# One encoder layer on one core: elementwise work taken from GpSimd, low-rank products in full passes

## The chip, the core and the metric

One core of a Trainium2 chip runs the whole layer as one program. Its engines work side by side, each on its own queue of instructions in order: TensorE (PE, with its weight loads PEld), VectorE (DVE), ScalarE (ACT), GpSimd (POOL) and SyncE (SP), which issues the DMAs. The metric is the device time of one execution in microseconds. Before the change it is 4108.12 us, median of three runs (4107.86 to 4108.83).

## The reference, cut to what matters

Two sequences (2048 and 256 tokens, width 1024, float32) run through one layer: RMSNorm, one projection to 3328 columns, half of which feed differential attention and half a two-directional RWKV-7 recurrence, an output projection and a squared-ReLU MLP. The parts that the change touches:

```python
q = apply_rope(rms_norm(q, q_norm_g), cos, sin)          # the same for k
p = softmax(q k^T * scale)                               # two maps per head
attn = p[:, :, 0] - lam * p[:, :, 1]; o = attn @ v

zf = zf + mu_prev * (z_prev - zf) + mu_next * (z_next - zf)
w_log = -softplus(-(w0 + tanh(w_dn) @ w_up)) - 0.5;  decay = exp(-exp(w_log))
a_rate = sigmoid(a0 + a_dn @ a_up);  g = sigmoid(g_dn) @ g_up
kk = k * k_k / norm(k * k_k);  k_dir = k * (1 + (a_rate - 1) * k_a)
# w_up, a_up: rank 64 to 512 channels, for two directions
# state = state * w_t + (state a_t) b_t + v_t k_t;  y = state r_t
bonus = sum(r * k_dir * r_k) * v
```

## The kernel before, in words

The 2304 tokens are 18 tiles of 128 rows. Four stages follow one another, with some overlap.

**Projection and mixer preparation (0 to about 1026 us).** `project_stream` walks over column groups of 256 in a fixed order. Every product is three float32r passes (`mm3`, lines 100 to 102: high by high, low by high, high by low). Mixer columns are made transposed (`tall`), attention columns with tokens on the partitions (`wide`, two token tiles at a time). A wide tile of q or k goes through `rope` (lines 325 to 373): squares on ScalarE, their sum on VectorE, the power -0.5 on GpSimd (`rsqrt`, line 90), the product with it on VectorE (qn), then the rotation: t1 on GpSimd (L346), one half of t2 on VectorE and one on GpSimd (L349), the sum (L353), a split into two parts (L355, L356), transposes on TensorE (L363) and the stores. Tiles qn, t1 and the shared buffer of rsq and t2 are single, so one rope tile follows another.

Beside it `rw_prep` (line 717) prepares the recurrence for two token tiles at a time: nine blocks, each with four chunks of 128 channels. A block mixes neighbouring tokens (`mix`, L737 to L739), splits the 64 + 64 low-rank rows (wa) into a high and a low part (L747, L748) and, for each chunk and direction, multiplies them with w_up and a_up (L813): the w half on partitions 0 to 63, the a half on 64 to 127, three products of 64 rows for each. Tanh follows (L815), an affine map on GpSimd (L816), a running sum along time (L819), two exponentials (L822, L823), and the operands aro and kb of the recurrence: the products L831, L846, L847 and L853 and the map L844 on GpSimd, the rest on VectorE (L834, L841, L843, L854). Preparation steps are put between projection steps by a rate (PREP_RATE). Within a stage the order of the instructions on each engine is settled when the program is built, by a planner that simulates the engines with its own costs.

**Attention beside the recurrence (about 1026 to 2222 us).** `attn_stream` takes one head and one tile of 128 queries at a time; the long sequence has four blocks of 512 keys for each of the two maps. `attn_scores`: two score products (L601, L602) into one of three PSUM buffers, the row maximum on VectorE (L604), the exponential on ScalarE (L608). `attn_combine` brings the four blocks to one maximum: map 0 is rescaled, blocks 0 and 1 on ScalarE (L631), 2 and 3 on GpSimd (L633); map 1 is multiplied and added, blocks 0 and 2 in one VectorE operation (L639), 1 and 3 in two on GpSimd (L636, L637). `attn_pv` transposes and multiplies with the values one query tile later. The recurrence (`rw_units`: inter, leaf, merge, chain) is put between by a ratio; its leaf (L954, L956) has part of its steps on GpSimd.

**wout and MLP (2222 to 4106 us).** Not touched by the change.

Of the kernel before, what the change touches and what calls it, by code (L numbers as in the profile page):

```python
# [22 lines left out]
CDEC = -0.5 * float(np.exp(-0.5))  # L23
# [34 lines left out]
class K:  # L58
# [266 lines left out]
    def rope(self, ps, t, m, c0):  # L325

        nc, sp, pp = self.nc, self.pj, self.pjp
        CW = self.CW
        part, g0, n = c0 // 512, (c0 % 512) // 64, CW // 64
        gcs = sp.tile([128, m, 128], F32, name="gcs", tag="gcs")  # L330
        runs = [0] + [j for j in range(1, m) if self.pos[t + j] != self.pos[t + j - 1] + 1] + [m]
        for j0, j1 in zip(runs, runs[1:]):
            p0 = self.pos[t + j0] * 128
            nc.sync.dma_start(out=gcs[:, j0:j1], in_=self.cst[part, p0:p0 + (j1 - j0) * 128].rearrange("(n p) c -> p n c", p=128))
        sq = sp.tile([128, m * n, 64], F32, name="rsq", tag="rsq", bufs=RSQ)
        z = ps.rearrange("p m (a b) -> p (m a) b", b=64)
        nc.scalar.activation(out=sq, in_=z, func=AF.Square)
        ss = sp.tile([128, m * n], F32, name="rss", tag="rss")
        nc.vector.tensor_reduce(out=ss, in_=sq, axis=AX.X, op=ALU.add)
        rs = sp.tile([128, m * n], F32, name="rrs", tag="rrs")  # L340
        self.rsqrt(rs, ss, 1.0 / 64, 1e-6)
        qn = sp.tile([128, m * n, 64], F32, name="qn", tag="qn", bufs=1)
        nc.vector.tensor_tensor(out=qn, in0=z, in1=rs.unsqueeze(2).to_broadcast([128, m * n, 64]), op=ALU.mult)  # L343
        t1 = sp.tile([128, m, n, 64], F32, name="t1", tag="t1", bufs=1)
        q4 = qn.rearrange("p (m a) b -> p m a b", m=m)
        nc.gpsimd.tensor_tensor(out=t1, in0=q4, in1=gcs[:, :, 0:64].unsqueeze(2).to_broadcast([128, m, n, 64]), op=ALU.mult)  # L346
        t2 = sp.tile([128, m, n, 64], F32, name="t2", tag="rsq", bufs=RSQ)
        for s in range(2):
            (nc.vector, nc.gpsimd)[T2E[s]].tensor_tensor(  # L349
                out=t2[:, :, :, 32 * s:32 * s + 32], in0=q4[:, :, :, 32 - 32 * s:64 - 32 * s],  # L350
                in1=gcs[:, :, 64 + 32 * s:96 + 32 * s].unsqueeze(2).to_broadcast([128, m, n, 32]), op=ALU.mult)
        hl = sp.tile([128, m * n, 2, 64], F32R, name="hl", tag="hl", bufs=1)
        nc.vector.tensor_tensor(out=t1, in0=t1, in1=t2, op=ALU.add)  # L353
        t1 = t1.rearrange("p m a b -> p (m a) b")
        nc.scalar.copy(hl[:, :, 0], t1)  # L355
        nc.vector.tensor_tensor(out=hl[:, :, 1], in0=t1, in1=hl[:, :, 0].bitcast(F32), op=ALU.subtract)  # L356

        def transposes():
            hT = sp.tile([128, n, m, 128], F32R, name="hlT", tag="hlT", bufs=1)
            for j in range(m):  # L360
# [12 lines left out]
        return transposes
# [343 lines left out]
    def rw_prep(self, seq, b0, n):  # L717
# [25 lines left out]
        wa = sp.tile([128, W], F32, name="wa", tag="wa", bufs=1)  # L743
        mix(zr, 0, 12, wa)
        nc.scalar.activation(out=wa[0:64], in_=wa[0:64], func=AF.Tanh)
        xh, xl = (sp.tile([128, W], F32R, name="wa" + s, tag="wa" + s, bufs=1) for s in ("hi", "lo"))
        nc.scalar.copy(xh, wa)  # L747
        nc.vector.tensor_tensor(out=xl, in0=wa, in1=xh.bitcast(F32), op=ALU.subtract)  # L748
        zg = sp.tile([128, W], F32, name="zg", tag="wa", bufs=1)
        mix(zr, 1, 13, zg)  # L750
        nc.scalar.activation(out=zg, in_=zg, func=AF.Tanh, scale=0.5)
        nc.gpsimd.tensor_scalar(out=zg, in0=zg, scalar1=0.5, scalar2=0.5, op0=ALU.mult, op1=ALU.add)
        nc.sync.dma_start(out=self.SG[:, ts], in_=zg)
        yield
        kf = sp.tile([128, 4, W], F32, name="kf", tag="kf", bufs=1)
# [48 lines left out]
        for c in range(4):  # L804
# [1 line left out]
            lw = sp.tile([128, 2, W], F32, name="lw", tag="lw", bufs=LWB)  # L806
            th = sp.tile([128, 2, W], F32, name="th", tag="th", bufs=2)
            for d in range(2):
                ps = [pp.tile([128, W], F32, name="aps", tag="w512") for _ in range(2)]
                for i, (wt, x) in enumerate(((0, xh), (0, xl), (1, xh))):  # L810
                    for k in range(2):
                        ks = slice(k * 64, k * 64 + 64)
                        nc.tensor.matmul(ps[k], self.rpw[wt][ks, d, c * 128:c * 128 + 128], x[ks], start=i == 0, stop=i == 2)  # L813
                for p, o, bias in zip(ps, (lw[:, 1, ::-1] if d else lw[:, 0], th[:, d]), (self.w0h, self.a0h)):
                    nc.scalar.activation(out=o, in_=p, func=AF.Tanh, scale=0.5, bias=bias[:, d * 4 + c:d * 4 + c + 1])  # L815
            nc.gpsimd.tensor_scalar(out=lw, in0=lw, scalar1=CDEC, scalar2=CDEC, op0=ALU.mult, op1=ALU.add)  # L816
            eg, en = self.eg, sp.tile([128, 2, W], F32, name="en", tag="en", bufs=ENB)
            l2 = lw.rearrange("p d t -> p (d t)")
            nc.vector.tensor_tensor_scan(out=l2, data0=self.chunk[:, 0:2 * W], data1=l2, initial=0.0, op0=ALU.mult, op1=ALU.add)  # L819
            for d in range(2):  # L820
                x = lw[:, 1, ::-1] if d else lw[:, 0]
                nc.scalar.activation(out=eg[:, d, 0:nq, 1:65], in_=x.rearrange("p (q t) -> p q t", t=64), func=AF.Exp)  # L822
                nc.scalar.activation(out=en[:, d], in_=x, func=AF.Exp, scale=-1.0)  # L823
                e = 1 if d else 64
                nc.gpsimd.tensor_copy(self.pcs[:, s0 + b0:s0 + b0 + n, d, c], eg[:, d, 0:nq, e:e + 1].rearrange("p (j x) o -> p j (x o)", x=2))
            rf = sp.tile([128, W], F32, name="rf", tag="rf", bufs=1)
            mix(zrr, c, c, rf)
            kq = kk[:, c].rearrange("p (q t) -> p q t", t=64)
            nc.vector.scalar_tensor_tensor(out=kk[:, c], in0=kf[:, c], scalar=self.k_k[:, cs], in1=rsb[:, c], op0=ALU.mult, op1=ALU.mult)
            ar = sp.tile([128, nq, 2, 2, 64], F32, name="aro", tag="aro", bufs=1)  # L830
            nc.gpsimd.tensor_tensor(out=ar[:, :, :, 1].rearrange("p q d t -> p d q t"), in0=rf.rearrange("p (q t) -> p q t", t=64).unsqueeze(1).to_broadcast([128, 2, nq, 64]),  # L831
                                    in1=eg[:, :, 0:nq, 1:65], op=ALU.mult)
            for d in range(2):
                nc.vector.scalar_tensor_tensor(out=ar[:, :, d, 0], in0=kq[:, :, ::-1] if d else kq, scalar=-0.5,  # L834
# [4 lines left out]
            for d in range(2):  # L839
# [1 line left out]
                nc.vector.scalar_tensor_tensor(out=b[:, :, ::-1] if d else b, in0=th[:, d].rearrange("p (q t) -> p q t", t=64), scalar=1.0, in1=kq, op0=ALU.add, op1=ALU.mult)  # L841
                e = en[:, d].rearrange("p (q t) -> p q t", t=64)
                nc.vector.tensor_tensor(out=b, in0=b, in1=e[:, :, ::-1] if d else e, op=ALU.mult)  # L843
            nc.gpsimd.tensor_scalar(out=th, in0=th, scalar1=self.ka2[:, cs], scalar2=self.ka1[:, cs], op0=ALU.mult, op1=ALU.add)  # L844
            kd = th
            nc.gpsimd.tensor_tensor(out=kd, in0=th, in1=kf[:, c:c + 1].to_broadcast([128, 2, W]), op=ALU.mult)  # L846
            nc.gpsimd.tensor_tensor(out=bk[:, :, :, 0].rearrange("p q d t -> p d q t"), in0=kd.rearrange("p d (q t) -> p d q t", t=64), in1=en.rearrange("p d (q t) -> p d q t", t=64), op=ALU.mult)  # L847
            dst = self.BK[:, qs, :, c].rearrange("p q d k -> p (q d) k")
            nc.sync.dma_start(out=dst[64:128], in_=bk[64:128].rearrange("p q d s t -> p (q d) (s t)"))
            for z in range(2):  # L850
                nc.sync.dma_start(out=dst[0:64, :, 64 - 64 * z:128 - 64 * z], in_=bk[0:64, :, :, z].rearrange("p q d t -> p (q d) t"))
            bo = sp.tile([128, W], F32, name="kds", tag="ksq")
# [19 lines left out]

    def rw_prep_weights(self):
        nc = self.nc
        raw = self.rp.tile([128, 2, 512], F32, name="a_raw", tag="kf", bufs=1)
        for h, nm in enumerate(("w_up", "a_up")):
            nc.sync.dma_start(out=raw[h * 64:h * 64 + 64], in_=self.I[nm].rearrange("d r c -> r d c"))
        hi, lo = self.rpw = [self.rp.tile([128, 2, 512], F32R, name="up" + s, bufs=1) for s in ("hi", "lo")]
        nc.scalar.copy(hi, raw)
        nc.vector.tensor_tensor(out=lo, in0=raw, in1=hi.bitcast(F32), op=ALU.subtract)  # L880
        self.chunk = self.rp.tile([128, 512], mybir.dt.bfloat16, name="chunk", bufs=1)
        nc.gpsimd.memset(self.chunk, 1.0)
        nc.gpsimd.memset(self.chunk[:, ::64], 0.0)
# [313 lines left out]
D0E = "gpsimd"  # L1197
WB = 2
ARE = ("scalar", "scalar")
STP = (1, 3)  # L1200
PA = 6
PB = 6
PAIR0 = 2
DACO = [512, 1024, 768, 1280, 0, 256]
PAIR1 = 2
T2E = (0, 1)
KDE = 1
YPT = "w"
SCP = False
MORD = "icm"  # L1210
RUN0 = False
HPS = ""
SCA = (0, 1)
LFV = 14
AT = 2
XNB = 2
# [95 lines left out]
```

## Time and profile before

The profiled execution took 4107.6 us; its span is 4105.8 us.

| engine | busy us | share of the span |
|---|---|---|
| PE | 3914.7 | 95% |
| PEld | 3460.1 | 84% |
| DVE | 2468.3 | 60% |
| ACT | 1896.3 | 46% |
| POOL | 1293.7 | 32% |

The shares are means over stages with different limits, so the stages are read one by one. "Busy" of PE counts a product until its modelled end; products start before the one ahead has ended, so the distance of two starts tells their cost better. The releaser behind an arrow is the instruction that ended an idle time.

### The profile page before, as it was taken

What the parts mean: (1) busy time and instruction counts of PE and PEld (TensorE: products, weight loads), DVE (VectorE), ACT (ScalarE), POOL (GpSimd) and SP (SyncE); (2) the same over time, 40 slices, a digit from 0 to 9 for tenths busy, and PEclk for the clock granted to TensorE, in tenths of its full rate; (3) what the DMA queues carried; (4) which work ended last, traced back from release to release, by engine and by line L of the source; (5) the groups of instructions that cost most, each with busy time, mean ns of one, the idle gap of its engine ahead of it and who ended that gap; (6) DMA issues with size and microseconds to landing.
All of it is one profiled execution on the core that took longest, in us unless ns stands there. A gap on an engine that the chain in (4) does not pass through costs nothing.

```text
span 4105.8 us, 75582 instructions
## 1 busy us (share of the span) xinstructions
PE 3914.7 (95%) x28790; PEld 3460.1 (84%) x28790; DVE 2468.3 (60%) x4770; ACT 1896.3 (46%) x4343; POOL 1293.7 (32%) x1822
## 2 busy tenths in 40 slices
PE   7999997997989999999997999999999999999999
PEld 7999887886777777787776788999999999999998
DVE  4244788777867777777785775444444444444443
ACT  4343454444766767676775224333333333333332
POOL 0033666666555656565564440000000000000000
PEclk9999998998999999999998999999999999999999
DMA  7565776656335335334324376222152222422111
GB/s 236 203 217 178 224 217 196 199 171 171 84 93 144 80 96 131 89 89 132 91 65 140 109 233 205 62 69 66 62 185 62 64 66 65 156 62 62 62 62 39
DMA packets 614588, 506.57 MB, mean 123 GB/s; under 512 B 250632, under 2 KB 543440, under 8 KB 607568
## 3 DMA queue, kind: packets, MB, share of 16 engines
q1 hardware_dynamic: 614224, 501.73, 41.5%
q8 instruction: 227, 3.72, 0.4%
q14 instruction: 137, 1.12, 0.1%
HBM read 336.41 MB, written 165.17 MB: 122 GB/s over the span
## 4 chain that ended last, share of the span: by engine, by line
PE 60%; DVE 6%; DMA 4%; POOL 2%; ACT 1%; issue 1%; SPq 1%; DVEq 0%; POOLq 0%; ACTq 0%
PE ups L100 7%; PE ups L101 7%; PE ups L102 7%; PE yps L102 6%; PE yps L101 6%; PE yps L100 6%; PE oo L650 4%; PE scp L928 3%; PE sc L601 2%; PE atp L645 2%; PE wops L101 2%; PE sc L602 2%; PE wops L102 2%; PE wops L100 2%; DVE nb L604 1%; DVE ltmp L954 1%
## 5 line engine op out<-in xcount | busy, mean ns | idle before, releaser
L517 DVE TENSOR_TENSOR acc<-yps,acc 128x512 f32<-128x512 f32 x576 | 392.1, 688 | 379.0 <-PE yps L102 378.9
L100 PE MATMUL ups<-h2hi,f_hi 128*128 128x384 f32 x1536 | 520.3, 339 | 0.0
L101 PE MATMUL ups<-h2lo,f_hi 128*128 128x384 f32 x1536 | 520.2, 339 | 0.0
L102 PE MATMUL ups<-h2hi,f_lo 128*128 128x384 f32 x1536 | 519.8, 338 | 0.0
L101 PE MATMUL yps<-f_lo,uh 128*128 128x512 f32 x1152 | 450.8, 392 | 0.0
L100 PE MATMUL yps<-f_hi,uh 128*128 128x512 f32 x1152 | 448.8, 390 | 0.0
L102 PE MATMUL yps<-f_hi,ul 128*128 128x512 f32 x1152 | 444.6, 393 | 0.0
L604 DVE TENSOR_REDUCE nb<-sc 128x1 f32<-128x512 f32 (+1 forms) x528 | 346.7, 675 | 145.6 <-PE sc L602 143.8
L608 ACT ACTIVATE P<-sc,nb 128x512 f32<-128x512 f32 (+1 forms) x528 | 360.0, 685 | 145.5 <-DVE nb L604 142.6
L137 ACT CAST f_hi<-f_raw 128x1024 fp32r<-128x1024 f32 x96 | 96.1, 1046 | 648.2 <-PE yps L102 646.9
L650 PE MATMUL oo<-vv,at 128*128 128x128 f32 x2080 | 301.6, 290 | 10.1 <-ACT o L662 6.5
L101 PEld LDWEIGHTS ups<-h2lo,f_hi 128*128 128x128 f32 x1536 | 288.2, 188 | 6.3
L100 PEld LDWEIGHTS ups<-h2hi,f_hi 128*128 128x128 f32 x1536 | 288.3, 188 | 5.9
L102 PEld LDWEIGHTS ups<-h2hi,f_lo 128*128 128x128 f32 x1536 | 288.2, 188 | 5.5
L505 DVE TENSOR_TENSOR ul<-u,uh 128x384 fp32r<-128x384 f32 x192 | 106.9, 557 | 307.5 <-ACT uh L504 303.9
L650 PEld LDWEIGHTS oo<-vv,at 128*128 128x128 f32 x2080 | 264.0, 196 | 32.2 <-ACT o L662 8.1
L100 PE MATMUL mm<-w_hi,hT_hi 128*128 128x256 f32 x864 | 260.1, 302 | 20.9 <-DVE qn L343 18.6
L601 PE MATMUL sc<-kt,qq 128*128 128x512 f32 (+1 forms) x528 | 244.6, 463 | 19.3 <-ACT P L608 17.4
L102 PE MATMUL mm<-w_hi,hT_lo 128*128 128x256 f32 x864 | 258.6, 299 | 0.0
L101 PE MATMUL mm<-w_lo,hT_hi 128*128 128x256 f32 x864 | 258.6, 299 | 0.0
L102 PEld LDWEIGHTS yps<-f_hi,ul 128*128 128x128 f32 x1152 | 216.1, 188 | 46.7
L143 DVE SCALAR_TENSOR_TENSOR f_lo<-f_raw,g,f_hi 128x256 fp32r<-128x256 f32 x384 | 168.5, 481 | 142.2 <-ACT f_hi L142 142.2
(236 smaller groups left out, 9334.7 us busy)
## 6 DMA issues: line engine op xcount, KB each, us to landing
f_raw<-w_ff SPq DMA_DIRECT2D x192, 256.0 KB, 2.8
f_raw<-w_ff SPq DMA_DIRECT2D x96, 512.0 KB, 3.4
AR<-aro SPq DMA_DIRECT2D x36, 512.0 KB, 3.8
qq<-QT SPq DMA_DIRECT2D x288, 64.0 KB, 2.4
ar<-AR SPq DMA_DIRECT2D x36, 512.0 KB, 4.5
bk<-BK SPq DMA_DIRECT2D x36, 512.0 KB, 3.9
ZT<-zs SPq DMA_DIRECT2D x84, 192.0 KB, 3.3
xt<-x SPq DMA_DIRECT2D x27, 512.0 KB, 5.3
```

Of the source, the lines that this page charges most:

```text
L100: mm(ps, lh, rh, start=start, stop=False)
L101: mm(ps, lh, rl, start=False, stop=False)
L102: mm(ps, ll, rh, start=False, stop=stop)
L137: nc.scalar.copy(hi[:, ks], raw)
L143: nc.vector.scalar_tensor_tensor(out=lo[:, k], in0=raw[:, k - k0], scalar=gk, in1=hi[:, k].bitcast(F32), op0=ALU.mult, op1=ALU.subtract)
L505: nc.vector.tensor_tensor(out=ul[:, ns], in0=u2, in1=uh[:, ns].bitcast(F32), op=ALU.subtract)
L517: nc.vector.tensor_tensor(out=acc[j][:, cs], in0=ps, in1=acc[j][:, cs], op=ALU.add)
L601: nc.tensor.matmul(sc, qq[:, c, 0], kt, start=True, stop=False)
L604: nc.vector.tensor_reduce(out=m, in_=sc, axis=AX.X, op=ALU.max, negate=True)
L608: nc.scalar.activation(out=P, in_=sc, func=AF.Exp, bias=m, accum_out=(a["ls"][:, hf] if a["nh"] > 1 else a["l"])[:, c:c + 1])
L650: nc.tensor.matmul(a["op"], at[:, b], a["kv"][1][hf][:, b], start=k == 0, stop=k == a["n"] - 1)
L928: nc.tensor.matmul(ps[:, c], bk[hs, c, x].rearrange("p s t -> p (s t)"), ar[hs, c, x].rearrange("p s t -> p (s t)"), start=True, stop=True)
```

## The change

The rope products t1 and the second half of t2 go to VectorE (T2E = (0, 0)). In the preparation the products L831, L846, L847 and the sum L853 go to VectorE; the affine maps L752, L816, L844 and the copy L825 to ScalarE. In attention all four rescalings of map 0 are on ScalarE (SCA) and all four products of map 1 on VectorE (STP is empty). The low-rank operands are laid out anew: w_up and a_up have each their own tile with the high part on partitions 0 to 63 and the low part on 64 to 127; xs holds the high part of the input twice, xl its low part above zeros, so that two products of 128 rows give what three of 64 rows gave. The products of one direction share one PSUM tile.

```diff
-        nc.gpsimd.tensor_tensor(out=t1, in0=q4, in1=gcs[:, :, 0:64]..., op=ALU.mult)
+        nc.vector.tensor_tensor(out=t1, in0=q4, in1=gcs[:, :, 0:64]..., op=ALU.mult)
...
-        xh, xl = (sp.tile([128, W], F32R, name="wa" + s, tag="wa" + s, bufs=1) for s in ("hi", "lo"))
-        nc.scalar.copy(xh, wa)
-        nc.vector.tensor_tensor(out=xl, in0=wa, in1=xh.bitcast(F32), op=ALU.subtract)
+        xs, xl = sp.tile([128, 2, W], F32R, name="xs", tag="xs", bufs=1), self.xl
+        for k in range(2):
+            x = wa[k * 64:k * 64 + 64]
+            for p in (0, 64):
+                nc.scalar.copy(xs[p:p + 64, k], x)
+            nc.vector.tensor_tensor(out=xl[0:64, k, 0:W], in0=x, in1=xs[k * 64:k * 64 + 64, k].bitcast(F32), op=ALU.subtract)
...
-        nc.gpsimd.tensor_scalar(out=zg, in0=zg, scalar1=0.5, scalar2=0.5, op0=ALU.mult, op1=ALU.add)
+        nc.scalar.activation(out=zg, in_=zg, func=AF.Copy, scale=0.5, bias=0.5)
...
-                ps = [pp.tile([128, W], F32, name="aps", tag="w512") for _ in range(2)]
-                for i, (wt, x) in enumerate(((0, xh), (0, xl), (1, xh))):
-                    for k in range(2):
-                        ks = slice(k * 64, k * 64 + 64)
-                        nc.tensor.matmul(ps[k], self.rpw[wt][ks, d, c * 128:c * 128 + 128], x[ks], start=i == 0, stop=i == 2)
-                for p, o, bias in zip(ps, (lw[:, 1, ::-1] if d else lw[:, 0], th[:, d]), (self.w0h, self.a0h)):
-                    nc.scalar.activation(out=o, in_=p, func=AF.Tanh, scale=0.5, bias=bias[:, d * 4 + c:d * 4 + c + 1])
-            nc.gpsimd.tensor_scalar(out=lw, in0=lw, scalar1=CDEC, scalar2=CDEC, op0=ALU.mult, op1=ALU.add)
+                ps = pp.tile([128, 2, W], F32, name="aps", tag="w512")
+                for k, o, bias in ((0, lw[:, 1, ::-1] if d else lw[:, 0], self.w0h), (1, th[:, d], self.a0h)):
+                    for x in (xs, xl):
+                        nc.tensor.matmul(ps[:, k], self.rpw[k][:, d, c * 128:c * 128 + 128], x[:, k, 0:W], start=x is xs, stop=x is xl)
+                    nc.scalar.activation(out=o, in_=ps[:, k], func=AF.Tanh, scale=0.5, bias=bias[:, d * 4 + c:d * 4 + c + 1])
+            nc.scalar.activation(out=lw, in_=lw, func=AF.Copy, scale=CDEC, bias=CDEC)
...
-            nc.gpsimd.tensor_scalar(out=th, in0=th, scalar1=self.ka2[:, cs], scalar2=self.ka1[:, cs], op0=ALU.mult, op1=ALU.add)
+            nc.scalar.activation(out=th, in_=th, func=AF.Identity, scale=self.ka2[:, cs], bias=self.ka1[:, cs])
...
+        for nm in ("w_up", "a_up"):
+            raw = self.rp.tile([64, 2, 512], F32, name="a_raw", tag="kf", bufs=1)
+            nc.sync.dma_start(out=raw, in_=self.I[nm].rearrange("d r c -> r d c"))
+            w = self.rp.tile([128, 2, 512], F32R, name=nm, bufs=1)
+            nc.scalar.copy(w[0:64], raw)
+            nc.vector.tensor_tensor(out=w[64:128], in0=raw, in1=w[0:64].bitcast(F32), op=ALU.subtract)
+            self.rpw.append(w)
+        self.xl = self.rp.tile([128, 2, 256], F32R, name="xl", bufs=1)
+        nc.gpsimd.memset(self.xl[64:128].bitcast(F32), 0.0)
...
-STP = (1, 3)
+STP = ()
-T2E = (0, 1)
+T2E = (0, 0)
-SCA = (0, 1)
+SCA = (0, 1, 2, 3)
```

The other moved lines (L825 to ScalarE, L831, L846, L847, L853 to VectorE) change only the engine's name.

## Rows read from the trace of the kernel before

**Rows 1.** Busy time by stage: sum and count of each engine, clock, DMA share
```profile
0.00:308.00 308.00, 285.48 (x1644) 275.72 (x1645) 111.54 (x234) 119.85 (x262) 44.49 (x68) 0.99 0.67 219
308.00:924.00 616.00, 558.38 (x3936) 519.21 (x3935) 442.18 (x766) 285.16 (x680) 382.84 (x366) 0.94 0.66 197
924.00:1026.00 102.00, 76.53 (x472) 65.32 (x471) 71.55 (x121) 43.73 (x105) 66.39 (x73) 0.83 0.60 171
1026.00:2222.00 1196.00, 1130.58 (x13357) 931.83 (x13357) 892.75 (x2084) 830.93 (x2103) 688.32 (x1226) 0.97 0.39 97
```
**Rows 2.** Chain of waits by line: attention, then its first 200 us alone
```profile
by line: PE oo L650 11.9%; PE scp L928 9.7%; PE sc L601 6.7%; PE atp L645 5.7%; PE sc L602 5.3%; DVE nb L604 4.9%; DVE ltmp L954 4.0%; DVE lx L956 3.4%; issue 3.2%; PE yp L1008 3.0%; DMA lm<-MD 2.9%; DVE P L639 2.8%; DMA XD<-lx 2.6%; PE bp 
...
by line: PE scp L928 8.0%; DVE nb L604 7.5%; DMA XD<-lx 6.6%; PE oo L650 6.0%; DVE ltmp L954 5.3%; DVE lx L956 4.8%; issue 4.5%; POOL ltmp L954 4.3%; POOL lx L956 4.3%; DVE P L639 4.1%; POOL P L637 4.0%; PE sc L601 3.1%; PE atp L645 3.0%; D
```
**Rows 3.** Timeline of TensorE, a lone lot: start us, us, instruction
```profile
640.44 0.28 PE L102 MATMUL mm<-w_hi,hT_lo 128*128 128x256 f32 x1
640.65 0.38 PE L813 MATMUL aps<-wahi,uphi 64*128 64x256 f32 x1
...
641.42 0.28 PE L101 MATMUL mm<-w_lo,hT_hi 128*128 128x256 f32 x1
641.54 0.28 PE L102 MATMUL mm<-w_hi,hT_lo 128*128 128x256 f32 x1
```
**Rows 4.** Timeline of TensorE, two lots in one place
```profile
922.23 0.39 PE L813 MATMUL aps<-wahi,uphi 64*128 64x256 f32 x2
...
923.02 0.28 PE L102 MATMUL mm<-w_hi,hT_lo 128*128 128x256 f32 x1
```
**Rows 5.** GpSimd by line, 308 to 1026: busy us, mean ns, idle before, releasers
```profile
L90 POOL TENSOR_TENSOR rrs<-rrs,halfneg 128x8 f32<-128x8 f32 x32 | 56.5, 1766 | 43.6 <-DVE rrs L89 38.4 <-DVE nt_rs L89 4.8
...
L831 POOL TENSOR_TENSOR aro<-rf,eg 128x512 f32<-128x512 f32 x32 | 45.2, 1412 | 9.2 <-DVE rf L739 9.2
```
**Rows 6.** VectorE by line, 308 to 1026, first and last of 21 groups
```profile
L819 DVE TENSOR_TENSOR_SCAN lw<-chunk,lw 128x512 f32<-128x512 bf16 x32 | 45.9, 1433 | 6.5 <-POOL lw L816 6.5
...
L748 DVE TENSOR_TENSOR walo<-wa,wahi 128x256 fp32r<-128x256 f32 x7 | 3.9, 558 | 0.6 <-ACT wahi L747 0.6
```
**Rows 7.** Single lines of VectorE: ns minimum/median/maximum, first and last start
```profile
L819 DVE TENSOR_TENSOR_SCAN lw<-chunk,lw x36: 1209/1217/2299, 255.8 to 937.7; 128x512 f32<-128x512 bf16 x36
...
L353 DVE TENSOR_TENSOR t<-t,t x40: 409/692/1768, 462.7 to 1005.7; 128x512 f32<-128x512 f32 x32, 128x256 f32<-128x256 f32 x8
...
L748 DVE TENSOR_TENSOR walo<-wa,wahi x9: 410/415/1414, 192.1 to 861.4; 128x256 fp32r<-128x256 f32 x9
```
**Rows 8.** Timeline, all engines: a GpSimd and a VectorE operation side by side
```profile
767.64 1.46 POOL L346 TENSOR_TENSOR t<-qn,gcs 128x512 f32<-128x512 f32 x1
...
767.87 1.51 DVE L349 TENSOR_TENSOR t<-qn,gcs 128x256 f32<-128x256 f32 x1
```
**Rows 9.** Timeline of VectorE, one rope tile late in the first stage
```profile
966.02 0.68 DVE L339 TENSOR_REDUCE rss<-rsq 128x8 f32<-128x512 f32 x1
...
969.39 0.42 DVE L349 TENSOR_TENSOR t<-qn,gcs 128x256 f32<-128x256 f32 x1
971.69 0.69 DVE L353 TENSOR_TENSOR t<-t,t 128x512 f32<-128x512 f32 x1 [1.88 <-POOL t L349]
...
973.73 0.68 DVE L339 TENSOR_REDUCE rss<-rsq 128x8 f32<-128x512 f32 x1
```
**Rows 10.** Groups by line in attention, 1026 to 2222, columns as above
```profile
L637 POOL TENSOR_TENSOR P<-P,P 128x512 f32<-128x512 f32 x124 | 163.6, 1338 | 0.4
...
L636 POOL TENSOR_SCALAR P<-P,g 128x512 f32<-128x512 f32 x124 | 127.1, 1035 | 26.6 <-DVE g L626 23.0 <-ACT P L608 1.4
...
L639 DVE SCALAR_TENSOR_TENSOR P<-P,g,P 128x512 f32<-128x512 f32 x124 | 112.0, 941 | 4.1 <-POOL P L633 1.4
...
L631 ACT ACTIVATE P<-P,cf 128x512 f32<-128x512 f32 x124 | 83.0, 716 | 1.5
```
**Rows 11.** Waits, 308 to 1026: total us, times, longest us
```profile
POOL th L844 <- DVE kb L841: 33.5, 23, 4.9
```

More of the change, by code (lines that the diff above doesn't have):

```diff
@@ L345, in rope @@
         q4 = qn.rearrange("p (m a) b -> p m a b", m=m)
-        nc.gpsimd.tensor_tensor(out=t1, in0=q4, in1=gcs[:, :, 0:64].unsqueeze(2).to_broadcast([128, m, n, 64]), op=ALU.mult)
+        nc.vector.tensor_tensor(out=t1, in0=q4, in1=gcs[:, :, 0:64].unsqueeze(2).to_broadcast([128, m, n, 64]), op=ALU.mult)
         t2 = sp.tile([128, m, n, 64], F32, name="t2", tag="rsq", bufs=RSQ)
@@ L824, in rw_prep @@
                 e = 1 if d else 64
-                nc.gpsimd.tensor_copy(self.pcs[:, s0 + b0:s0 + b0 + n, d, c], eg[:, d, 0:nq, e:e + 1].rearrange("p (j x) o -> p j (x o)", x=2))
+                nc.scalar.copy(self.pcs[:, s0 + b0:s0 + b0 + n, d, c], eg[:, d, 0:nq, e:e + 1].rearrange("p (j x) o -> p j (x o)", x=2))
             rf = sp.tile([128, W], F32, name="rf", tag="rf", bufs=1)
@@ L830, in rw_prep @@
             ar = sp.tile([128, nq, 2, 2, 64], F32, name="aro", tag="aro", bufs=1)
-            nc.gpsimd.tensor_tensor(out=ar[:, :, :, 1].rearrange("p q d t -> p d q t"), in0=rf.rearrange("p (q t) -> p q t", t=64).unsqueeze(1).to_broadcast([128, 2, nq, 64]),
+            nc.vector.tensor_tensor(out=ar[:, :, :, 1].rearrange("p q d t -> p d q t"), in0=rf.rearrange("p (q t) -> p q t", t=64).unsqueeze(1).to_broadcast([128, 2, nq, 64]),
                                     in1=eg[:, :, 0:nq, 1:65], op=ALU.mult)
@@ L843, in rw_prep @@
                 nc.vector.tensor_tensor(out=b, in0=b, in1=e[:, :, ::-1] if d else e, op=ALU.mult)
-            nc.gpsimd.tensor_scalar(out=th, in0=th, scalar1=self.ka2[:, cs], scalar2=self.ka1[:, cs], op0=ALU.mult, op1=ALU.add)
+            nc.scalar.activation(out=th, in_=th, func=AF.Identity, scale=self.ka2[:, cs], bias=self.ka1[:, cs])
             kd = th
-            nc.gpsimd.tensor_tensor(out=kd, in0=th, in1=kf[:, c:c + 1].to_broadcast([128, 2, W]), op=ALU.mult)
-            nc.gpsimd.tensor_tensor(out=bk[:, :, :, 0].rearrange("p q d t -> p d q t"), in0=kd.rearrange("p d (q t) -> p d q t", t=64), in1=en.rearrange("p d (q t) -> p d q t", t=64), op=ALU.mult)
+            nc.vector.tensor_tensor(out=kd, in0=th, in1=kf[:, c:c + 1].to_broadcast([128, 2, W]), op=ALU.mult)
+            nc.vector.tensor_tensor(out=bk[:, :, :, 0].rearrange("p q d t -> p d q t"), in0=kd.rearrange("p d (q t) -> p d q t", t=64), in1=en.rearrange("p d (q t) -> p d q t", t=64), op=ALU.mult)
             dst = self.BK[:, qs, :, c].rearrange("p q d k -> p (q d) k")
@@ L852, in rw_prep @@
             bo = sp.tile([128, W], F32, name="kds", tag="ksq")
-            nc.gpsimd.tensor_tensor(out=bo, in0=kd[:, 0], in1=kd[:, 1], op=ALU.add)
+            nc.vector.tensor_tensor(out=bo, in0=kd[:, 0], in1=kd[:, 1], op=ALU.add)
             nc.vector.scalar_tensor_tensor(out=bo, in0=rf, scalar=self.r_k[:, cs], in1=bo, op0=ALU.mult, op1=ALU.mult)
@@ L874, in rw_prep_weights @@
         nc = self.nc
[L875 to L880, printed above, removed]
+        self.rpw = []
+        for nm in ("w_up", "a_up"):
[7 more added lines that the diff above has]
+        nc.gpsimd.memset(self.xl[64:128].bitcast(F32), 0.0)
         self.chunk = self.rp.tile([128, 512], mybir.dt.bfloat16, name="chunk", bufs=1)
```

## The prediction

> **What bounds the kernel now.** I read the busy times by stage first, because the change touches two stages only: the projection with its mixer preparation (0 to about 1026 us) and attention beside the recurrence (1026 to 2222). wout and the MLP (2222 to 4106) hold none of the edited lines, and I cost them at zero. In 308 to 924 TensorE is busy 558 of 616 us, VectorE 442, GpSimd 383, ScalarE 285; from 924 to 1026 TensorE falls to 77 of 102 with the granted clock at 0.83 [rows 1]. In attention TensorE is busy 1131 of 1196 us, VectorE 893, ScalarE 831, GpSimd 688 [rows 1]. Next the chain of waits in attention: its longest lines are TensorE's (oo, scp, sc, atp, sc, yp: 42.3%), then VectorE's nb, ltmp, lx and P (15.1%) and two DMAs; in its first 200 us GpSimd has a part too, P L637 with 4.0% and the leaf lines with 4.3% each [rows 2]. So TensorE leads in both stages, in neither alone: what it waits for comes from an ordered VectorE queue.
>
> **Low-rank products (first stage).** Before, each (block, chunk, direction) issues six products of 64 rows, in lots of three. A plain projection product follows the last one after 0.12 us. A lone lot runs from the projection product at 640.44 to the second one after it at 641.42: 0.98 us, of which two projection intervals are 0.24, so the lot costs 0.74 [rows 3]: three products at 0.12 and the rest lost where the engine goes from 128 rows to 64 and back. Where the lots of both halves come together (the records read x2) both cost 0.79 - 0.12 + 0.09 = 0.76 [rows 4]. I counted the 144 lots in the timeline: 103 stand alone, 19 places hold two, one holds three: 103 x 0.74 + 19 x 0.76 + 1.9 = 93 us. After: 9 blocks x 4 chunks x 2 directions x 4 = 288 products of full height at 0.12 = 35 us. TensorE loses 58 us of work. Sixteen lone lots lie before 308, where TensorE is busy 285 of 308 [rows 1]: 16 x 0.74 less 32 x 0.12 is 8 us, all taken. Of the other 50 I take four fifths, 40, since TensorE is 91% busy there; ends 0 (the wait only moves) and 50.
>
> The trace shows pairs at the price of one lot, and single lots at the same price. The Trainium skill, TensorEngine Tiling (Array Packing), section Key Properties, says that separate tiles work in parallel and that changing the tiling mode drains the engine. By its first half the six products would cost three slots, 72 x 3 x 0.12 = 26 us, and the full passes would be 9 us dearer; this holds in 19 places [rows 4], not in 103 [rows 3], so I go by the rows, which also show the second half (0.98 us for what five intervals of 0.12 would fill in 0.60).
>
> **Work put on VectorE (first stage).** A 512-column operation with both inputs in SBUF has a median of 692 ns, a 256-column one 415 [rows 7]. Added: t1 for 32 double and 8 single tiles, 32 x 0.69 + 8 x 0.42 = 25; second half of t2, 32 x 0.42 + 8 x 0.3 = 16; three operations for each of 36 chunks (aro, kd, kb), 108 x 0.69 = 75; the sum kds, 36 x 0.42 = 15; one more half-height subtraction per block, 4. Sum 135 us. Against it stands what the present operations lose beside GpSimd: the scan has a mean of 1433 ns and a median of 1217, walo 558 against 415 [rows 6, 7]; the same subtraction over the 21 groups from the first of these to the last gives 112 us. One place shows how: t on GpSimd runs 1.46 us from 767.64, and VectorE's 256-column t, begun at 767.87, takes 1.51 [rows 8] where the same operation takes 0.42 at 969.39 [rows 9]. GpSimd keeps the powers (rrs alone 56.5 us [rows 5]), some 95 of its 449 us here, so I credit 0.78 x 112 = 87. Net +48 us: 514 of 718 becomes 562 of about 660, 85% instead of 72%. I charge 10 us for longer queues; ends 0 and 48 (every added microsecond on the path).
>
> The trace shows the longer one ending with the other engine's. The Trainium skill, SBUF — State Buffer, section Who interferes with whom, gives the rule: a VectorE instruction with two SBUF inputs and a GpSimd one that reads SBUF exclude each other. By that rule the credit would go on into attention, which is the third rival below.
>
> **Work put on ScalarE (first stage).** 72 affine maps of 512 columns at 0.72 (P L631 [rows 10]) = 52 us; 72 tiny copies, 27 half-height ones and 9 maps of 256 columns at half of that, 39. Hidden: ScalarE goes from 285 to some 370 of 616 us. The map of th now waits on ScalarE for kb: GpSimd spent 33.5 us in 23 such waits [rows 11]. Queued behind it there are the next tanhs, the hT_hi, hl and hlT casts and the evictions that TensorE needs. The 10 us above cover it; its upper end is 33 more. The moved lw map follows its tanh on the same engine, so a hand-over goes.
>
> **Rope tiles at the ends of the column groups.** In the last column pair each rope tile waits for the one before it: reduction at 966.02, the next at 973.73, 7.7 us; from VectorE's t at 969.39 to the sum at 971.69 the path is GpSimd's two products, 1.88 us of it waiting [rows 9]. After: 0.69 + 0.42 + 0.42 on VectorE instead of 2.3 + 0.07 from the end of qn, about 0.9 us less per tile, which is down to TensorE's share of a tile (48 products x 0.12 = 5.8 and eight transposes). Some 8 tiles here and 10 in the pair at 640 to 720: 16 us, value 15 with the clock that comes back; ends 0 and 25. First stage: -8 - 40 + 10 - 15 = -53.
>
> **Attention.** GpSimd loses 164 + 127 us of P lines [rows 10] and the two rescalings. VectorE gets 124 more P operations at 0.69, 86 us, and its own 124 fall from 0.94 towards 0.69 [rows 7, 10], 31 back; the leaf and S operations give perhaps 20 more. Net +35: 928 of 1196. ScalarE gets 124 x 0.716 = 89: 920 of 1196. The last block of a row is no longer two GpSimd operations of 1.04 + 1.34 us in a queue but one of 0.69 [rows 10]; TensorE needs it only one tile later, so I take -15. Ends: -60 and +89 (both rivals below).
>
> **At nothing:** two weight loads in turn instead of one at the start (under TensorE's first products; a few us if the cover goes), the cleared half of xl, the shared PSUM tile. No transfer inside the loops is moved on SP's queue.
>
> **Sum:** -53 - 15 = -68 on the profiled execution's 4107.6 us (span 4105.8; median of the runs 4108.12, half a microsecond more): 4040.
>
> **Rivals.**
> 1. VectorE becomes the bound of the first stage and the added 48 us are on the path; attention gains nothing: -8 - 40 + 48 - 15 = -15, 4092. For it: VectorE at 85%. Against: the median durations are reached only without GpSimd, which is what the edit gives.
> 2. Slower: ScalarE in attention. Two more rescalings, 1.43 us, stand between the exponentials of one tile and those of the next, and three score buffers are all that lets TensorE run on. On the 62 long query tiles of this stage 89 us, so -53 + 89 = +36: 4144. It decides from 53 / 62 = 0.86 us of added stall per tile on. For it: 920 of 1196 busy, one queue in order. Against: ScalarE still has 276 us idle, 4.5 us per tile, and hardly stands on the chain [rows 2].
> 3. More: GpSimd's interference is what delays the chain. ltmp, lx and P are 10.2% of 1196, 122 us; a quarter of that (0.94 to 0.69) is 30, and GpSimd's P lines on the chain give as much: -60. First stage at its good ends, -8 - 50 - 25 = -83. Sum -143: 3965. Against: the leaf stays on GpSimd.
>
> **Chances.** Forecast 0.58, own range 4010 to 4070; rival 1 0.15; rival 2 0.12; rival 3 0.15. Range 3965 to 4115: below lies half of rival 3's spread, above most of rival 2. A change of 0.2%, 8 us, is about the least that a measurement of this kernel tells from none. Faster: 0.56 + 0.09 + 0.15 = 0.80; within 0.2%: 0.07; slower: 0.13.
>
> **What would show it.** Right: aps products with no mark of the row change, 0.12 us apart, 288 of them; P L639 and t1 near 0.69 us; attention starting 40 to 60 us earlier and lasting about 1180. Wrong: VectorE near full in 308 to 924 with TensorE waiting for qn, hl or kds (rival 1); TensorE's sc waiting for ScalarE's P, attention over 1240 (rival 2); attention under 1150 (rival 3). The order of instructions is planned anew for the whole stage, which could move any of these by tens of us.

## The result and the profile after

The changed kernel takes 4035.26 us (median of four runs, 4026.77 to 4036.21) against 4108.48 of the kernel before on the same chip (four runs, 4107.86 to 4109.98): a ratio of 0.9818, 95% interval 0.9807 to 0.983, 73 us less. Its profiled execution took 4034.81 us, span 4032.6; forecast 4040. A few executions took thousands of us longer (one each of e6, e11 and e12 below) and are left out of every median.

Busy time by stage, after, columns and windows as in [rows 1]:

```profile
0.00:308.00 308.00, 285.30 (x1676) 281.74 (x1677) 120.99 (x259) 132.00 (x294) 16.89 (x36) 0.97 0.67 220
308.00:924.00 616.00, 560.12 (x4077) 544.08 (x4075) 466.12 (x1030) 358.83 (x884) 92.07 (x63) 0.93 0.72 213
924.00:1026.00 102.00, 82.22 (x529) 67.68 (x530) 74.29 (x179) 64.81 (x157) 13.42 (x30) 0.85 0.44 120
1026.00:2222.00 1196.00, 1127.37 (x13334) 927.26 (x13334) 898.11 (x2175) 880.35 (x2162) 362.71 (x866) 0.97 0.41 106
```

GpSimd's busy time falls from 383 to 92 us in 308 to 924. VectorE runs 264 instructions more there for 24 us more. These windows cut the two kernels at different points of their work, so I cut each at its own marks: the first wide product (mm on w_hi and hT_hi, L100) and the first and last product with the values (oo, L650). Single lines, columns engine, operation, tile, count, ns minimum/median/maximum, first and last start. Before:

```profile
L100 PE MATMUL mm<-w_hi,hT_hi x864: 274/283/583, 443.9 to 981.8; 128*128 128x256 f32 x173
...
L650 PE MATMUL oo<-vv,at x2080: 270/275/583, 1010.4 to 2219.0; 128*128 128x128 f32 x190
```

After:

```profile
L100 PE MATMUL mm<-w_hi,hT_hi x864: 274/283/582, 426.2 to 930.5; 128*128 128x256 f32 x173
...
L650 PE MATMUL oo<-vv,at x2080: 270/275/583, 955.4 to 2147.3; 128*128 128x128 f32 x190
```

Attention starts 55 us earlier (1010.4 to 955.4; forecast 53) and lasts 1191.9 instead of 1208.6, 17 us less (forecast 15); the rest of the span changes by 1.5 us. Inside the first stage 18 us are gained before the first wide product and 34 in the wide stretch, from the first wide product to the last (537.9 to 504.3 us). Its busy times, before and then after:

```profile
443.90:981.80 537.90, 469.93 (x3472) 437.92 (x3472) 416.70 (x702) 249.16 (x582) 366.09 (x340) 0.92 0.67 196
```

```profile
426.20:930.50 504.30, 449.81 (x3407) 434.24 (x3406) 403.52 (x900) 302.32 (x734) 88.96 (x63) 0.91 0.72 211
```

VectorE does 198 instructions more in this stretch and is busy 13 us less (and 11 us more ahead of it, 178.4 to 189.2). Groups of VectorE up to the last wide product (line, engine, operation, tiles, shapes, count, busy us, mean ns, idle before and its releasers), before:

```profile
L143 DVE SCALAR_TENSOR_TENSOR w_lo<-w_raw,g,w_hi 128x256 fp32r<-128x256 f32 x104 | 59.6, 611 | 75.3 <-ACT w_hi L142 75.2
L819 DVE TENSOR_TENSOR_SCAN lw<-chunk,lw 128x512 f32<-128x512 bf16 x36 | 50.7, 1409 | 7.5 <-POOL lw L816 7.5
...
L843 DVE TENSOR_TENSOR kb<-kb,en 128x256 f32<-128x256 f32 x72 | 39.8, 574 | 0.1
```

After:

```profile
L143 DVE SCALAR_TENSOR_TENSOR w_lo<-w_raw,g,w_hi 128x256 fp32r<-128x256 f32 x104 | 46.1, 481 | 78.6 <-ACT w_hi L142 78.6
L820 DVE TENSOR_TENSOR_SCAN lw<-chunk,lw 128x512 f32<-128x512 bf16 x36 | 43.9, 1218 | 8.1 <-ACT lw L817 8.1
...
L844 DVE TENSOR_TENSOR kb<-kb,en 128x256 f32<-128x256 f32 x72 | 28.5, 416 | 0.3
...
L847 DVE TENSOR_TENSOR th<-th,kf 128x512 f32<-128x512 f32 x36 | 24.7, 686 | 4.5 <-ACT th L845 4.4
```

The scan's mean is now 1218 ns, about the median of before [rows 7], where its mean was 1409 (1433 in [rows 6], from 308 on); the moved product kd (L847) costs 0.69 us. TensorE around the low-rank products, after (start us, us, instruction), beside [rows 3, 4]:

```profile
242.48 0.33 PE L102 MATMUL mm<-hT_hi,w_lo 128*128 128x384 f32 x1
242.65 0.28 PE L815 MATMUL aps<-xs,w_up 128*128 128x256 f32 x1
242.77 0.28 PE L815 MATMUL aps<-xl,w_up 128*128 128x256 f32 x1
242.89 0.34 PE L100 MATMUL mm<-hT_hi,w_hi 128*128 128x384 f32 x1
```

They stand 0.12 us apart with nothing lost at either end. All 288 products are there, and behind 216 of them the next one starts within 0.12 us. The Trainium skill, TensorEngine Tiling (Array Packing), section Key Properties, says that changing the tiling mode drains the engine; with no change of mode left, no gap is left, which agrees.

### The profile page after: what moved, and what is told of

Read it like the earlier page. It is cut to its first block, busy times and chain, and to the rows that moved or that the text cites. A ratio compares the mean times of both kernels' runs of the same rounds, so it can differ in the third digit from the quotient of the medians.

```text
span 4032.6 us, 75020 instructions
## 1 busy us (share of the span) xinstructions
PE 3861.2 (96%) x28646; PEld 3444.1 (85%) x28646; DVE 2458.1 (61%) x5132; ACT 2033.0 (50%) x4652; POOL 568.6 (14%) x1062
## 4 chain that ended last, share of the span: by engine, by line
PE 73%; DMA 9%; DVE 7%; ACT 5%; POOL 2%; SPq 2%; issue 2%; DVEq 0%; ACTq 0%; POOLq 0%
PE ups L100 7%; PE ups L101 7%; PE ups L102 7%; PE yps L102 7%; PE yps L101 7%; PE yps L100 7%; PE oo L650 4%; PE scp L933 3%; PE mm L100 3%; PE mm L102 3%; PE mm L101 3%; PE sc L601 2%; PE atp L645 2%; PE sc L602 2%; PE wops L100 2%
## 5 line engine op out<-in xcount | busy, mean ns | idle before, releaser
L100 PE MATMUL ups<-h2hi,f_hi 128*128 128x384 f32 x1536 | 520.3, 339 | 0.0
L100 PE MATMUL yps<-f_hi,uh 128*128 128x512 f32 x1152 | 448.8, 390 | 0.0
L650 PE MATMUL oo<-vv,at 128*128 128x128 f32 x2080 | 303.9, 291 | 16.5 <-ACT at L647 13.4
L650 PEld LDWEIGHTS oo<-vv,at 128*128 128x128 f32 x2080 | 265.6, 198 | 40.9 <-ACT at L647 20.8
L100 PEld LDWEIGHTS ups<-h2hi,f_hi 128*128 128x128 f32 x1536 | 288.3, 188 | 5.9
L100 PE MATMUL mm<-w_hi,hT_hi 128*128 128x256 f32 x864 | 259.8, 301 | 18.7 <-DVE qn L343 11.1
L142 ACT ACTIVATE f_hi<-f_raw,g 128x256 fp32r<-128x256 f32 x384 | 168.9, 500 | 171.2 <-PE ups L101 110.5
```

The costliest lines, as they stand in the source:

```text
L100: mm(ps, lh, rh, start=start, stop=False)
L142: nc.scalar.activation(out=hi[:, k], in_=raw[:, k - k0], func=AF.Copy, scale=gk)
L650: nc.tensor.matmul(a["op"], at[:, b], a["kv"][1][hf][:, b], start=k == 0, stop=k == a["n"] - 1)
```

## The experiments

Four kernels do one part of the change each, on the kernel before.

**e1: only the low-rank products.**

```diff
-                for i, (wt, x) in enumerate(((0, xh), (0, xl), (1, xh))):   # 64 rows, two halves
...
+                    for x in (xs, xl):                                      # 128 rows
```

> The kernel before with only the low-rank products in two full passes (288 products of 128 rows for 432 of 64); all elementwise work stays where it was. Theory (TensorE's work in the first stage is what counts, and row changes are its hidden part): the first stage shortens by 35 to 55 us, 4055 to 4075 us in all, attention as long as before. Rival (VectorE beside GpSimd sets the first stage's pace, TensorE has slack): under 15 us, above 4093.

4100.94 us against 4107.64: 0.9981 (0.997 to 0.9992), 7 us. The theory missed; the time lies where the rival has it. The marks of e1, in the same two windows (to its first wide product, and the wide stretch):

```profile
0.00:425.90 425.90, 399.68 (x2366) 392.00 (x2367) 176.71 (x354) 173.68 (x401) 100.17 (x127) 1.00 0.68 218
425.90:971.90 546.00, 456.23 (x3388) 443.90 (x3387) 426.83 (x715) 259.07 (x610) 367.68 (x344) 0.88 0.66 194
```

The first wide product comes 18 us earlier, as much as in the whole change. The wide stretch is then 8 us longer than before (546.0 against 537.9): TensorE is busy 14 us less, idle 22 us more, and its granted clock (a mean over its levels of 1.2 and 2.4 GHz) is 0.88 instead of 0.92. TensorE's own work doesn't set that stretch. Its longest waits in e1, 308 to 960 us (engine, line, waited for, total us, times, longest):

```profile
PE cps L797 <- DVE kds L855: 31.2, 15, 5.1
PE mm L100 <- DVE qn L343: 25.0, 12, 4.6
```

Both are for VectorE. The same two in the kernel before, 308 to 1015 us:

```profile
PE mm L100 <- DVE qn L343: 18.6, 12, 2.9
PE cps L794 <- DVE kds L854: 10.5, 10, 2.3
```

And in the kernel after, 308 to 960 us:

```profile
PE mm L100 <- DVE qn L343: 11.1, 9, 3.5
PE cps L797 <- DVE kds L855: 9.3, 9, 2.7
```

**e2: only the rope products.**

```diff
-        nc.gpsimd.tensor_tensor(out=t1, in0=q4, ...
+        nc.vector.tensor_tensor(out=t1, in0=q4, ...
...
-T2E = (0, 1)
+T2E = (0, 0)
```

> The kernel before with only the rope products t1 and t2 on VectorE. Theory: rope tiles at the ends of the column groups get about 0.9 us shorter each; 10 to 20 us less, 4090 to 4098. Rival (the longer VectorE queue takes it back, as GpSimd is still busy with the preparation and still interferes): 4105 to 4125.

4099.87 us: 0.9979 (0.9967 to 0.9991), 8 us, just outside the theory's range. Its first wide product is already 4.6 us earlier (439.3 against 443.9), ahead of every rope tile, so part of this comes from the order planned anew. By its products with the values, attention starts 15 us earlier (1010.4 to 995.4); some 5 us are lost again behind this mark, where the edit changes nothing:

```profile
L650 PE MATMUL oo<-vv,at x2080: 270/275/583, 995.4 to 2205.7; 128*128 128x128 f32 x190
```

**e3: only the preparation's moves** (L831, L846, L847, L853 to VectorE; L752, L816, L825, L844 to ScalarE).

```diff
-            nc.gpsimd.tensor_tensor(out=kd, in0=th, ...
+            nc.vector.tensor_tensor(out=kd, in0=th, ...
...
-            nc.gpsimd.tensor_scalar(out=lw, in0=lw, ...
+            nc.scalar.activation(out=lw, in_=lw, func=AF.Copy, ...
```

> The kernel before with only the preparation's elementwise work moved (three products and a sum to VectorE, maps and the small copy to ScalarE). Theory: what VectorE gains by GpSimd's absence (112 us over its operations) about pays for what it gets (about 94 us); 0 to -15 us, 4093 to 4108. Rival (interference delayed the path, its end is a gain by itself): -25 us or more, below 4083. Other rival (VectorE becomes the bound): above 4115.

4062.88 us: 0.9892 (0.987 to 0.9913), 45 us, the largest part by far. The theory missed; this is the first rival's range. Its wide stretch:

```profile
435.10:938.50 503.40, 458.35 (x3495) 427.18 (x3494) 396.88 (x806) 294.21 (x704) 178.70 (x139) 0.95 0.71 209
```

This edit alone brings the stretch to the length that it has after the whole change (503.4 and 504.3 us), with the old low-rank products in it, and VectorE is busy 20 us less there than before while it does 104 instructions more (ahead of the stretch it is busy 14 us more).

**e4: only attention** (STP empty, SCA all four).

```diff
-STP = (1, 3)
+STP = ()
...
-SCA = (0, 1)
+SCA = (0, 1, 2, 3)
```

> The kernel before with only attention's combining moved (all four products of map 1 on VectorE, all rescalings on ScalarE). Theory: attention shortens by about 15 us, 4088 to 4098, with ScalarE's part of the chain growing. Rival (ScalarE's queue is too long): slower, above 4110. Rival (interference on the chain): -40 us or more.

4092.43 us: 0.996 (0.9944 to 0.9976), 15 us, the forecast term. The four parts add up to 75 us (7 + 8 + 45 + 15), the whole to 73. This agreement is in part chance, since the parts are not worth the same together: in their place the low-rank products are worth 21 us (e5), which leaves 53 to the other three and not 68.

**e5: the kernel after with the old low-rank products**, to price them in their place (the reverse of e1's diff).

> The changed kernel with the low-rank products as before (three passes of 64 rows). Theory now (low-rank passes shorten only the stretch up to the first wide product, where TensorE is the bound): 15 to 20 us of the change are lost there and little after, 4045 to 4055. Rival (once VectorE is free of GpSimd, TensorE is the bound in the later stretch too): 30 to 50 us lost, 4065 to 4085. Rival (nothing but noise, as 7 us alone): 4035 to 4043.

4056.29 us against 4109.7: 0.9873 (0.9858 to 0.9888), 21 us above the kernel after and 1 above the theory's range. By the marks of the profiled execution (4053.05 us), 9.7 of it lie before the first wide product (435.9 against 426.2) and 3.7 in the wide stretch (508.0 against 504.3); the rest is spread behind:

```profile
435.90:943.90 508.00, 466.89 (x3496) 435.37 (x3495) 394.27 (x879) 295.06 (x706) 86.55 (x62) 0.94 0.71 207
```

**e6 and e7: idle work on GpSimd.** Both are e5 with GpSimd work that nothing uses, after the operands of each chunk: e6 three products that read SBUF, e7 eight clears that only write it. A copy of one element per partition ties them to the chunk.

```diff
+            nc.gpsimd.tensor_copy(self.dm[:, 0, 0:1], en[:, 0, 0:1])   # e6, e7
+            for _ in range(3):
+                nc.gpsimd.tensor_tensor(out=self.dm, in0=self.dm, in1=self.ident..., op=ALU.mult)   # e6
...
+            for _ in range(8):
+                nc.gpsimd.memset(self.dm, 1.0)   # e7
```

> e5_no_lowrank with three products of 512 columns more on GpSimd in each of the 36 chunks, on a tile that nothing else reads; they read SBUF and feed nobody, after one element taken from en ties them to the chunk. Theory (GpSimd's reads lengthen VectorE's two-input operations): the 256-column kb products of VectorE go from about 0.42 to over 0.5 us, and 20 to 45 us are added to e5_no_lowrank. Rival (what counted before was the wait for GpSimd's slow results): under 8 us added.

> e5_no_lowrank with eight 512-column clears on GpSimd instead, about the same GpSimd time and tied the same way, with nothing read from SBUF. Theory (reads against reads): VectorE's durations stay at about 0.42 us and under 8 us are added. Rival (any GpSimd work beside VectorE lengthens it, or the powers queued behind the added work delay the rope tiles): 20 us or more, as e6_idle_reads.

e6: 4115.69 us, 1.002 (1.0009 to 1.0031), 59 us above e5 (20 to 45 were expected) and slower than the kernel before. e7: 4047.72 us, 0.9852 (0.9835 to 0.9869), 9 us below e5, with intervals that overlap. Reads cost and writes don't, as the theory has it; the price of the reads was put too low. GpSimd spends the same time on both. The added group and one VectorE operation with two SBUF inputs, in e6, 0 to 1026 us:

```profile
L843 DVE TENSOR_TENSOR kb<-kb,en 128x256 f32<-128x256 f32 x72 | 37.7, 543 | 0.1
...
L850 POOL TENSOR_TENSOR dm<-dm,ident 128x512 f32<-128x512 f32 x108 | 153.8, 1424 | 7.9
```

And in e7:

```profile
L843 DVE TENSOR_TENSOR kb<-kb,en 128x256 f32<-128x256 f32 x72 | 28.7, 419 | 0.1
...
L850 POOL MEMSET dm<- 128x512 f32 x288 | 153.0, 531 | 15.8
```

154 us of reading raise kb from 419 to 543 ns; 153 us of writing leave it. One place in e6, the timeline of GpSimd and VectorE:

```profile
603.99 4.15 POOL L850 TENSOR_TENSOR dm<-dm,ident 128x512 f32<-128x512 f32 x3
604.12 1.45 DVE L738 SCALAR_TENSOR_TENSOR wa<-zr,mu_prev,wa 128x256 f32<-128x256 f32 x1
605.48 1.50 DVE L346 TENSOR_TENSOR t<-qn,gcs 128x256 f32<-128x256 f32 x1
606.90 1.58 DVE L349 TENSOR_TENSOR t<-qn,gcs 128x128 f32<-128x128 f32 x2
608.41 0.47 DVE L739 SCALAR_TENSOR_TENSOR wa<-zr,mu_next,wa 128x256 f32<-128x256 f32 x1
```

While GpSimd's three products run (603.99 to 608.14), each record of VectorE takes about as long as one of them (1.38 us); the next one takes 0.47 again. The Trainium skill, SBUF — State Buffer, section Who interferes with whom, says that a VectorE instruction with two SBUF inputs contends with a GpSimd one that reads SBUF and not with one that only writes it. e6 and e7 agree with both halves.

**e8: of e3 only the products and the sum on VectorE**, the maps left on GpSimd (e3's diff without its ScalarE lines).

> The kernel before with only the three products and the sum of each chunk on VectorE (aro, kd, kb, kds); maps and the small copy stay on GpSimd. Theory (the four reading operations make most of the interference): 25 to 40 us less, 4068 to 4083, most of e3_prep's 45. Rival (the hand-overs of lw, th and pcs were the delay): under 15 us less, above 4092.

4090.7 us: 0.9959 (0.9944 to 0.9974), 19 us, between theory and rival, both of which missed. 26 us of e3's 45 come only when the maps and copies leave as well. VectorE's groups in e8, 308 to 1026 us:

```profile
L819 DVE TENSOR_TENSOR_SCAN lw<-chunk,lw 128x512 f32<-128x512 bf16 x32 | 41.6, 1299 | 28.5 <-POOL lw L816 28.5
...
L843 DVE TENSOR_TENSOR kb<-kb,en 128x256 f32<-128x256 f32 x64 | 29.7, 488 | 0.1
```

The scan (1299 ns, 1218 after) and kb (488, 416 after) still lose time beside the maps, and the scan waits 28.5 us for GpSimd's map lw. But in e3 the scan waits 30.9 us for ScalarE's lw (308 to 1026 us), and VectorE is busy as long in e3's wide stretch (396.9 us in 503.4) as in e8's:

```profile
442.60:964.00 521.40, 475.29 (x3490) 444.17 (x3490) 396.56 (x795) 254.95 (x594) 248.82 (x240) 0.91 0.68 200
```

So neither longer operations nor this one wait explains the 26 us by itself; what makes them stays open.

**e9 to e11: GpSimd's part in attention.** On the kernel after: e9 puts the whole leaf on VectorE, e10 puts blocks 2 and 3 of map 0 back on GpSimd, e11 puts them on VectorE.

```diff
-LFV = 14
+LFV = 0                                              # e9
...
-SCA = (0, 1, 2, 3)
+SCA = (0, 1)                                         # e10, e11
...
-                    nc.gpsimd.tensor_scalar(out=A, in0=A, scalar1=cf[:, hf, 0:1], ...
+                    nc.vector.tensor_scalar(out=A, in0=A, scalar1=cf[:, hf, 0:1], ...   # e11
```

> The changed kernel with all steps of the recurrence's leaf on VectorE (none on GpSimd). Theory (in attention VectorE is now off the path, TensorE waits for ScalarE; GpSimd's leaf still interferes a little): within 10 us of the changed kernel, 4025 to 4045. Rival (the leaf on GpSimd still delays the chain, 62 us of it): 4010 to 4025. Rival (468 small operations of about 0.25 us more, 120 us, make VectorE the bound): above 4050.

> The changed kernel with the rescaling of blocks 2 and 3 back on GpSimd (all products stay on VectorE). Theory (ScalarE's queue is what TensorE waits for in attention, but each GpSimd rescaling reads SBUF beside VectorE): the two nearly cancel, 4025 to 4045. Rival (interference as in the first stage): 4050 or more. Rival (ScalarE's queue alone decides): below 4020.

> The changed kernel with the rescaling of blocks 2 and 3 on VectorE as a one-input operation. Theory (ScalarE on the chain, VectorE off it): ScalarE loses 124 x 0.71 = 88 us, VectorE gets 124 x about 0.45 = 56; 10 to 25 us less than the changed kernel, 4010 to 4025. Rival (VectorE at over 79% is as bad): 4035 to 4055.

e9: 4050.89 us, 0.9859 (0.9836 to 0.9881), 16 us above the kernel after; the theory missed. e10: 4034.22, 0.9822 (0.9804 to 0.9841), the same, as its theory has it. e11: 4041.34, 0.9837 (0.9817 to 0.9857), 6 us above with intervals that overlap; the theory (10 to 25 us less) missed. e9's attention, first to last oo:

```profile
955.60:2152.90 1197.30, 1124.81 (x13258) 942.71 (x13258) 964.15 (x2692) 904.09 (x2236) 164.96 (x398) 0.95 0.41 101
```

TensorE's longest wait there:

```profile
PE sc L601 <- ACT P L608: 24.9, 18, 4.2
```

With half of GpSimd's remaining time in attention gone (338 to 165 us), VectorE is 62 us busier (902.4 to 964.2), not freer; whether that or ScalarE's P makes the 16 us isn't shown. In e10 the products with the values take 11 us less (1180.7 against 1191.9), and what follows them takes 9 more, with 96 TensorE products more in it, so work has moved over this mark:

```profile
L650 PE MATMUL oo<-vv,at x2080: 270/275/583, 953.4 to 2134.1; 128*128 128x128 f32 x190
```

In the whole time, neither emptying GpSimd further nor easing ScalarE gains anything.

**e12: the low-rank pair issued twice**, 288 products of 0.12 us more, 35 us of added TensorE work.

```diff
-                    for x in (xs, xl):
+                    for x in (xs, xl, xs, xl):
```

> The changed kernel with each full-height low-rank pair issued twice (the second pair overwrites the first with the same values): 288 more products of 0.12 us, 35 us of TensorE work. Theory (TensorE's work counts up to the first wide product and hardly after it, where TensorE waits for other engines): the first wide product 8 to 12 us later, under 20 us in all, 4040 to 4055. Rival (TensorE is the bound of the whole first stage once GpSimd is off): 30 us or more, above 4065.

4039.76 us against 4106.99: 0.9846 (0.9822 to 0.987), 5 us above the kernel after (12 by the two ratios, whose intervals overlap), as the theory has it. Its wide stretch:

```profile
436.50:935.10 498.60, 454.53 (x3588) 441.87 (x3587) 394.37 (x879) 295.19 (x714) 87.37 (x62) 0.94 0.72 210
```

The first wide product comes 10 us later; the wide stretch with its 181 products more is 6 us shorter than after, at a granted clock of 0.94 instead of 0.91. VectorE has 21 instructions and 9 us less in it, which now stand ahead of the mark, so the products are not all that differs.

## Why the prediction was right, and where its steps were not

The forecast total and both of its stages held (55 for 53, 17 for 15). For the first stage this is luck: two of its terms were wrong by tens of us in opposite directions, and the errors cancelled.

**Low-rank, -8 and -40: too large.** Measured 7 alone (e1) and 21 in place (e5). The cost of a lot and of the two passes was read rightly. What failed is "of the other 50 I take four fifths, 40, since TensorE is 91% busy there": a busy share of 91% did not make TensorE the bound. Up to the first wide product its work does count. Of the 144 lots 48 lie there (32 alone, 8 pairs), 18 us at the prediction's prices, and the mark moved by 18 us in e1, by 9.7 in e5 and by 10 in e12; 8 had been counted, to 308 only. (e2 and e4, which change nothing ahead of this mark, move it by 4.6 and 4.7.) The other 40 us of saved work lie behind it, where TensorE waits for VectorE: in e1 they turned into idle time, beside a lower granted clock, and the products added in e12 cost nothing there.

**Work put on VectorE, +10: wrong in sign.** The net load was put at +48 us: 135 added less 87 credited. Up to the last wide product VectorE is busy 595.1 us before and 592.7 after. Summed by line up to attention's first product with the values, what was added takes 132 us (kd, aro and kb 0.68 to 0.69 each, as taken), and the operations that both kernels have take 127 less. So the credit should have been more than the whole of the 112 read from [rows 6, 7] and not 0.78 of it; w_lo (L143) alone lost 13.5 (59.6 us before, 46.1 after). And the loss lay on the path: the moves of the preparation alone are worth 45 us (e3), and giving GpSimd 154 us of reading back costs 59 (e6). So this, not the low-rank products, is the main gain. Rival 3 had its mechanism, but in the wrong stage.

**Rope tiles, -15: right per tile, wrong in number.** Reductions of three tiles in a row, after, beside [rows 9]:

```profile
884.11 0.68 DVE L339 TENSOR_REDUCE rss<-rsq 128x8 f32<-128x512 f32 x1
...
890.98 0.68 DVE L339 TENSOR_REDUCE rss<-rsq 128x8 f32<-128x512 f32 x1
...
897.84 0.68 DVE L339 TENSOR_REDUCE rss<-rsq 128x8 f32<-128x512 f32 x1
```

The distance is 6.9 us instead of 7.7: 0.8 less, 0.9 forecast. But of the 39 distances in the kernel before only two that follow a full tile are under 8 us (the others 8.4 to 21); "some 8 tiles here and 10 in the pair" took the rest for back to back, and in the pair, 640 to 720, only five reductions start, 11 to 21 us apart. So e2's gain (8 us, 15 at the start of attention) is not the step as argued. In its wide stretch VectorE does 77 instructions more for 6 us more (416.7 to 422.8), so there too its operations got shorter; what of the gain comes from that isn't shown.

**Attention, -15: held, with VectorE and ScalarE changing place.** The chain of waits by line, after, first to last oo, beside the first row of [rows 2]:

```profile
by line: PE oo L650 15.1%; PE scp L933 9.8%; PE sc L601 8.2%; PE atp L645 6.8%; PE sc L602 6.2%; PE yp L1013 4.7%; ACT P L608 4.1%; PE qp L1049 3.0%; issue 2.8%; POOL lx L961 2.7%; ACT P L631 2.6%; POOL ltmp L959 2.6%; DMA ar<-AR 2.3%; PE b
```

VectorE's nb, ltmp, lx and P have left the front of it, and ScalarE's P lines (6.7%) have come. VectorE's load rose by 2 us (900.6 to 902.4, first to last oo) and not by 35: P L639 takes 67 more, where 55 were taken, and the leaf's ltmp and lx alone 37 less, where 20 were taken with S. ScalarE's rose by 69 (836.8 to 905.9; 89 forecast). P L639 has a median of 0.75 us, not the 0.69 taken from another operation:

```profile
L639 DVE SCALAR_TENSOR_TENSOR P<-P,g,P x264: 459/746/949, 931.7 to 2130.0; 128x512 f32<-128x512 f32 x128, 128x256 f32<-128x256 f32 x4
```

ScalarE's rescalings, after, 956 to 2147 us:

```profile
L631 ACT ACTIVATE P<-P,cf 128x512 f32<-128x512 f32 x250 | 160.6, 713 | 1.5
```

TensorE's longest wait in the same stretch:

```profile
PE sc L601 <- ACT P L608: 13.0, 9, 4.4
```

Before, that wait was 10.1 us in eight times: rival 2's mechanism is there and costs 3 us, not 89. Taking the two rescalings off ScalarE again gains nothing in the whole time (e10). At 1192 us attention lies outside what either rival said of it (over 1240, under 1150).

**Rival 1** (VectorE the bound) was right that TensorE waits for VectorE in the wide stretch and wrong that the stretch would get longer, since VectorE's load did not grow.

**Open:** which part of e3's 45 us is interference and which hand-overs (e8), and the 5 to 10 us by which a newly planned order seems to move any of these kernels (the 4.6 and 4.7 of e2 and e4 ahead of the first wide product; e7 below e5).

## What to carry to other kernels

Compare the mean of each VectorE operation that reads two SBUF tiles with its undisturbed duration: the excess beside a reading GpSimd is real time of VectorE, and moving GpSimd's work over can cost VectorE next to nothing in sum (132 us added, 127 gone). Before crediting an engine with saved work, cut the stage at marks of its own and ask whom that engine waits for there; 91% busy was not enough. A gain per tile counts only where the tiles stand back to back, so list their distances first.

## What was not expected of the hardware

- The same GpSimd time costs 59 us as reading products (153.8 us, e6) and nothing that shows as clears (153.0 us, e7).
- Where TensorE wasn't the bound, its granted clock went with its work: 0.92 to 0.88 over the wide stretch in e1, where it was idle 22 us more, and 0.91 to 0.94 when products were added in e12. What this cost or gave in time wasn't measured.
- For 512 columns a scalar_tensor_tensor with two SBUF inputs took 746 ns (median, after) and a tensor_tensor 686 (mean, after); a tensor_scalar with one took 481 (median, e11):

```profile
L633 DVE TENSOR_SCALAR P<-P,cf x128: 470/481/709, 930.9 to 2126.7; 128x512 f32<-128x512 f32 x128
```
